# Latent attention heads: normalising the output rows instead of the exponentials, and moving the fp16 split from VectorE to ScalarE and GpSimd

## The chip, the core and the metric

The program runs on one core of one Trainium2 chip. A core has five engines with queues of their own, each strictly in order: TensorE (PE in the profile; its weight loads are shown apart as PEld), VectorE (DVE), ScalarE (ACT), GpSimd (POOL) and SyncE (SP), which here issues nearly all DMAs. They meet only at semaphores. The metric is the device time of one execution in microseconds. Before the change it is 1346.02 us, the median of three runs (1341.62 to 1346.54).

## The reference

One encoder layer over 1024 positions and 1024 channels: adaLN modulation, a mixer and a gated MLP. The mixer has 8 heads of banded attention and 8 heads of latent attention. The change touches the latent heads only, which compute (cut to that part):

```python
q = rmsnorm(q, g_mla_q[l]);  k = rmsnorm(k, g_mla_k[l])          # 96 wide per head
q = concat([q[..., :64], rope(q[..., 64:], positions)]);  k = ...
s = einsum('bqhd,bkhd->bhqk', qi, k) * scale
s = where(key_chunk <= q_chunk, s, NEG_INF)                       # chunks of 64
p = softmax(s, axis=-1)
o = einsum('bhqk,bkhd->bqhd', p, v)                               # v is 64 wide per head
```

## The kernel before

Products are kept near fp32 accuracy by splitting operands into a high and a low half and multiplying three of the four pairs. For the attention weights both halves are fp16.

A *unit* is one head and one half (g = 0 or 1) of the 1024 query positions; the 8 latent heads give 16 units, named m00_0 (group 0, head 0, half 0), m00_1, m01_0 and so on to m13_1. A unit has four *rows*, query tiles of 128 positions; row i (0 to 7 over both halves of a head) looks at n = 128(i+1) keys. So rows 0 to 3 (half 0) have n of 128 to 512 and are *short*; rows 4 to 7 (half 1) have n of 640 to 1024, and their weights are split in two *pieces*, the first of 512 columns, the second of 128 to 512.

A unit starts with its **pages** (`qk_page`, L700, called by `mla_unit`, L915): TensorE transposes four 128x96 tiles of q into one PSUM bank, ScalarE copies the high half out, VectorE subtracts for the low half; then the same for k. The bank is a tile with the tag "T", of which there is one buffer (`TB = 1`, L43; `page_psum`, L694). A new tile of a tag waits until the readers of the tile before it are done, in the order in which the source asks for them. The eight PSUM banks are taken: two score tiles "S" of two banks each, one "T", one "pv" and two "mm" for other products.

`Unit.scores` (L742) does one row: matmuls into an S tile; VectorE masks with a memset (L789) and takes the row minimum of the negated scores (L790); ScalarE forms the exponentials and their row sum in one pass (L797, with a second instruction that reads the accumulator). VectorE turns the sum into 2^15/sum (L799, L800). For each piece GpSimd multiplies the exponentials by that factor and writes the high fp16 half (L73, the helper `scale_pool`), VectorE forms exponential times factor minus high half as the low half (L819), and SyncE issues one DMA that transposes both halves into a PT tile (L831).

`Unit.values` (L836) runs for every second row, three rows (`DEPTH`) behind the scores: matmuls of the value tiles against the transposed weights into the bank "pv" (L859). After the last pair of a unit ScalarE and VectorE add the two 64-row halves and undo the power-of-two scales (L868, L869), and SyncE stores the output (L873).

`pace` fills in other products between rows: first the up-projection of the second group of heads (`f_up(1)`, L596), then the part of the output projection that belongs to the banded heads (`f_oca`, L674). The source asks for things in the order of the loop at L984. The final order of each engine's queue is made at build time by a list scheduler from that order, with priorities raised for the scores (`OFF_S`), the split (`OFF_P`) and the values (`OFF_V`); it is then fixed.

Of the kernel before, what the change touches and what calls it, by code (L numbers as in the profile page):

```python
# [13 lines left out]
F32 = mybir.dt.float32  # L14
# [4 lines left out]
AF = mybir.ActivationFunctionType  # L19
ALU = mybir.AluOpType  # L20
AX = mybir.AxisListType
# [3 lines left out]
P = 128  # L25
# [18 lines left out]
MODE_C = "1111"  # L44
MODE_M = "1111"
# [19 lines left out]
def layer_kernel(ctx, tc, I, out):  # L65
# [6 lines left out]
    def scale_pool(o, i, s):  # L72
        pool.tensor_scalar(o, i, s, 1.0, op0=MUL, op1=MUL)  # L73
# [241 lines left out]
    def pow2_scale(nm, ssw, b2, n, fac):  # L315
        t = cst.tile([P, 3, ND], F32, name=f"vs{nm}")
        dve.tensor_tensor(t[:, 0, :n], ssw, b2, op=MUL)
        pt = ps.tile([P, 512], F32, name=f"vsp{nm}", tag="mm", bufs=2)
        pe.matmul(pt[:, :n], ones[:], t[:, 0, :n], start=True, stop=True)
        dve.tensor_reduce(t[:, 1, 0:1], pt[:, :n], axis=AX.X, op=ADD)  # L320
        dve.tensor_scalar(t[:, 1, 0:1], t[:, 1, 0:1], fac, 1e-30, op0=MUL, op1=ADD)
        pool.tensor_tensor(t[:, 1, 1:2], t[:, 1, 0:1], nhalf[:], op=ALU.pow)
        ab = cst.tile([P, 2], F32, name=f"vab{nm}")
        dve.tensor_scalar(t[:, 2, 0:1].bitcast(I32), t[:, 1, 1:2].bitcast(I32), 0x7F800000, None, op0=ALU.bitwise_and)
        dve.reciprocal(t[:, 2, 1:2], t[:, 2, 0:1])
        dve.tensor_scalar(t[:, 2, 1:2], t[:, 2, 1:2], 1.0001, None, op0=MUL)
        dve.tensor_scalar(t[:, 2, 1:2].bitcast(I32), t[:, 2, 1:2].bitcast(I32), 0x7F800000, None, op0=ALU.bitwise_and)
        dve.tensor_scalar(ab[:, 0:1], t[:, 2, 0:1], VSCALE, None, op0=MUL)
        dve.tensor_scalar(ab[:, 1:2], t[:, 2, 1:2], 1.0 / (VSCALE * PSCALE), None, op0=MUL)
        return ab[:, 0:1], ab[:, 1:2]  # L330
# [265 lines left out]
    def f_up(gr):  # L596
# [19 lines left out]
        vscale["m", gr] = pow2_scale(f"m{gr}", ssw[:], gb2[:], 1, float(KVR))  # L616
# [117 lines left out]
    class Unit:  # L734
# [7 lines left out]
        def scores(u, i):  # L742
# [6 lines left out]
            rsum = cst.tile([P, 1], F32, name=f"rs{nm}", tag="rsum", bufs=4)  # L749
            ri = cst.tile([P, 1], F32, name=f"ri{nm}", tag="ri", bufs=4)  # L750
            with tc.high_priority(offset=OFF_S):
# [36 lines left out]
                else:  # L788
                    dve.memset(sv[0:64, n - 64:n], BIG)  # L789
                    anchor["dve"] = dve.tensor_reduce(m[:], sv, axis=AX.X, op=MIN).ins  # L790
# [7 lines left out]
            with tc.high_priority(offset=OFF_P):  # L798
                dve.reciprocal(ri[:], rsum[:, 0:1])  # L799
                dve.tensor_scalar(ri[:], ri[:], PSCALE, None, op0=MUL)  # L800
                for x, (p0, p1) in enumerate(pieces):
# [7 lines left out]
                    mode = (MODE_C if u.band else MODE_M)[cnt[0] % 4]  # L809
                    if mode == "2":  # L810
                        scale_pool(pp, pp, ri[:])
                        act.activation(hl[:, :w], pp, AF.Copy)
                        pool.tensor_tensor(hl[:, w:2 * w], pp, hl[:, :w], op=SUB)
                    else:
                        if mode == "1":
                            scale_pool(hl[:, :w], pp, ri[:])
                        else:
                            act.activation(hl[:, :w], pp, AF.Copy, scale=ri[:])
                        dve.scalar_tensor_tensor(hl[:, w:2 * w], pp, ri[:], hl[:, :w], op0=MUL, op1=SUB)  # L819
# [12 lines left out]
                    for j in range(w // P):  # L832
                        where.setdefault(lo + p0 // P + j, []).append((b0 + j, b0 + j + w // P, i % 2))
            return sum(3 * max(107, w / 2.4) for _, _, w, _ in segs)

        def values(u, i):  # L836
# [17 lines left out]
            with tc.high_priority(offset=OFF_V):  # L854
# [7 lines left out]
                if i % 4 == 3:  # L862
# [6 lines left out]
                    dve.scalar_tensor_tensor(dst[r0], u.pv[r0], inv[r0], dst[r0], op0=MUL, op1=ADD)  # L869
                    if final:  # L870
# [735 lines left out]
```

## Time and profile before

| | before |
|---|---|
| median of the runs | 1346.02 us |
| profiled execution | 1345.89 us, span 1344.1 us |
| mean granted TensorE clock | 0.946 |
| PE busy | 1223.8 us (91%), 6168 instructions |
| VectorE busy | 1096.2 us (82%), 1928 |
| ScalarE busy | 622.7 us (46%), 1132 |
| GpSimd busy | 578.1 us (43%), 610 |

Busy time of PE is modelled from pipelined instructions, so a busy PE is not PE at its peak. In a group of instructions "out<-in xcount | busy, mean ns | idle before, releaser" gives the tiles that are written and read, how many instructions there were, their total and mean duration, and how long the engine stood idle just before them and whose work ended that. The latent heads take up the stretch from about 400 to 630 us of the span; the banded heads lie before it, the output projection and the MLP behind it.

### The profile page before, as it was taken

To read this page: it belongs to the slowest core of one execution; us is meant where nothing else is said; L and a number is where in the kernel's file an instruction comes from. 1 tells how busy PE (TensorE), PEld (TensorE's weight loads), DVE (VectorE), ACT (ScalarE), POOL (GpSimd) and SP (SyncE) were. 2 spreads that over 40 slices of the span, in tenths; PEclk is the share of its full clock that TensorE was granted. 3 is DMA by queue.
4 is the path that set the end of the run, shared out by engine and by line. 5 is a ranking of instruction groups with operands and counts; after the bars stand their busy time and mean duration, and the time that the engine had idled before them with its cause. 6 is when DMAs were issued, how large, how long until landed. Compare 5 with 4: busy or idle time off the path is not lost.

```text
span 1344.1 us, 18696 instructions
## 1 busy us (share of the span) xinstructions
PE 1223.8 (91%) x6168; PEld 1003.8 (75%) x6168; DVE 1096.2 (82%) x1928; ACT 622.7 (46%) x1132; POOL 578.1 (43%) x610
## 2 busy tenths in 40 slices
PE   4899798998877798886998999999999998999998
PEld 3788587896655567765776888888888886888886
DVE  6978798864679987894989988988899997687667
ACT  4453546443555544563376444444434444433431
POOL 5464557565646763354634444444445431000000
PEclk9899798998787889996999999999999998999999
DMA  8415577854413477779911333333323326943441
GB/s 323 138 35 116 135 177 179 192 127 110 87 32 80 94 153 165 141 150 252 377 49 47 126 110 133 103 122 98 133 102 118 126 98 241 390 141 117 130 161 63
DMA packets 223689, 190.57 MB, mean 142 GB/s; under 512 B 148708, under 2 KB 166884, under 8 KB 223592
## 3 DMA queue, kind: packets, MB, share of 16 engines
q1 hardware_dynamic: 223592, 189.38, 49.1%
q8 instruction: 48, 0.79, 0.2%
q14 instruction: 49, 0.40, 0.1%
HBM read 117.24 MB, written 37.49 MB: 115 GB/s over the span
## 4 chain that ended last, share of the span: by engine, by line
PE 41%; DVE 10%; issue 3%; ACT 2%; DMA 1%; POOL 1%; SPq 0%; DVEq 0%; ACTq 0%; POOLq 0%
PE p L1082 7%; PE p L1084 7%; PE p L1083 7%; PE dnA_P L1417 2%; PE dnA_P L1419 2%; PE dnA_P L1418 2%; PE dnB_P L1419 1%; PE dnB_P L1418 1%; PE dnB_P L1417 1%; DVE u L1253 1%; DVE u L1254 1%; PE op L154 1%; PE dnA L1417 1%; PE dnA L1419 1%; PE dnA L1418 1%
## 5 line engine op out<-in xcount | busy, mean ns | idle before, releaser
L77 ACT ACTIVATE dnP<-dnr 128x1024 fp32r<-128x1024 f32 x73 | 77.5, 1064 | 117.5 <-PE dnA_P L1419 46.4
L1391 DVE TENSOR_TENSOR dnP<-dnr,dnP 128x1024 fp32r<-128x1024 f32 x72 | 87.9, 1223 | 52.6 <-ACT dnP L77 52.6
L73 POOL TENSOR_SCALAR hlm<-Pm,rim 128x512 f16<-128x512 f32 (+3 forms) x96 | 68.8, 726 | 83.5 <-DVE rim L800 22.3
L84 POOL TENSOR_TENSOR wf<-wu,wf 128x512 fp32r<-128x512 f32 x22 | 38.8, 1762 | 116.3 <-ACT wf L77 116.3
L1253 DVE SCALAR_TENSOR_TENSOR u<-c,cvp,u 128x1023 f32<-128x1023 f32 x44 | 64.8, 1513 | 27.8 <-ACT u L1252 27.8
L73 POOL TENSOR_SCALAR hlc<-Pc,ric 128x640 f16<-128x640 f32 (+2 forms) x64 | 50.8, 797 | 61.0 <-ACT Pc L797 20.8
L819 DVE SCALAR_TENSOR_TENSOR hlm<-Pm,rim,hlm 128x512 f16<-128x512 f32 (+3 forms) x96 | 68.0, 719 | 9.8 <-POOL hlm L73 9.7
L797 ACT ACTIVATE Pc<-sc,mc 128x640 f32<-128x640 f32 (+2 forms) x64 | 42.1, 658 | 53.1 <-DVE mc L786 35.9
L797 ACT ACTIVATE Pm<-sm,mm 128x128 f32<-128x128 f32 (+3 forms) x64 | 47.1, 736 | 41.7 <-DVE mm L790 24.2
L84 POOL TENSOR_TENSOR wb<-wu,wb 128x512 fp32r<-128x512 f32 x22 | 38.1, 1732 | 64.5 <-ACT wb L77 50.7
L1252 ACT ACTIVATE u<-c,cvp 128x1024 f32<-128x1024 f32 x44 | 52.3, 1237 | 27.8 <-DVE c L1351 19.2
L1254 DVE SCALAR_TENSOR_TENSOR u<-c,cvp,u 128x1022 f32<-128x1022 f32 x44 | 63.8, 1488 | 0.0
L859 PE MATMUL pvm<-PTm,vt 128*128 128x256 f16 (+1 forms) x320 | 45.7, 294 | 17.0 <-DMA PTm<-hlm 9.9
L819 DVE SCALAR_TENSOR_TENSOR hlc<-Pc,ric,hlc 128x640 f16<-128x640 f32 (+2 forms) x64 | 51.6, 809 | 9.3 <-POOL hlc L73 8.7
L155 PE MATMUL ipq<-wq_s,hT 128*128 128x256 f32 x192 | 56.0, 292 | 0.1
L859 PEld LDWEIGHTS <-vt 128*128 128x128 f16 x320 | 31.6, 109 | 32.7 <-DMA PTm<-hlm 15.0
L154 PE MATMUL ipq<-wq_s,hT 128*128 128x256 f32 x192 | 55.8, 293 | 0.0
L156 PE MATMUL ipq<-wq_s,hT 128*128 128x256 f32 x192 | 55.4, 289 | 0.0
L77 ACT ACTIVATE wc<-ws 128x512 fp32r<-128x512 f32 x21 | 13.3, 632 | 88.0 <-DVE ws L1101 82.2
L1418 PE MATMUL dnA_P<-dnP 128*128 128x512 f32 x132 | 51.4, 389 | 0.0
L1419 PE MATMUL dnA_P<-dnP 128*128 128x512 f32 x132 | 51.3, 389 | 0.0
L1417 PE MATMUL dnA_P<-dnP 128*128 128x512 f32 x132 | 51.2, 389 | 0.0
(442 smaller groups left out, 4428.4 us busy)
## 6 DMA issues: line engine op xcount, KB each, us to landing
wu<-w_up SPq DMA_DIRECT2D x44, 512.0 KB, 3.5
dnr<-g_d SPq DMA_DIRECT2D x73, 256.0 KB, 2.8
aw<-w_ada SPq DMA_DIRECT2D x48, 256.0 KB, 3.5
g_d<-u SPq DMA_DIRECT2D x22, 512.0 KB, 3.0
dnr<-w_down SPq DMA_DIRECT2D x44, 256.0 KB, 5.3
adaw<-w_ada_a SPq DMA_DIRECT2D x16, 512.0 KB, 6.3
x<-x SPq DMA_DIRECT2D x16, 512.0 KB, 9.0
g_d<-gs SPq DMA_DIRECT2D x22, 256.0 KB, 2.8
```

The source lines that it names most:

```text
L73: pool.tensor_scalar(o, i, s, 1.0, op0=MUL, op1=MUL)
L77: act.activation(o, i, AF.Copy)
L797: act.activation(pr[:, :n], sv, AF.Exp, bias=m[:], scale=-1.0, accum_out=rsum[:, 0:1])
L819: dve.scalar_tensor_tensor(hl[:, w:2 * w], pp, ri[:], hl[:, :w], op0=MUL, op1=SUB)
L1082: pe.matmul(pt, sh, pg[:, 0], start=(k == 0 and not add), stop=False, skip_group_check=skip)
L1083: pe.matmul(pt, sh, pg[:, 1], start=False, stop=False, skip_group_check=skip)
L1084: last = pe.matmul(pt, sl, pg[:, 0], start=False, stop=(k == 3), skip_group_check=skip)
L1253: dve.scalar_tensor_tensor(u[:, 1:], c[:, :S - 1], cvp[:, cv + 1:cv + 2], u[:, 1:], op0=MUL, op1=ADD)
L1391: r = f(*a, **k)
L1417: pe.matmul(pt, sh, w[:, 0, 0], start=start, stop=False, skip_group_check=add)
L1418: pe.matmul(pt, sh, w[:, 1, 0], start=False, stop=False, skip_group_check=add)
L1419: pe.matmul(pt, sl, w[:, 0, 0], start=False, stop=stop, skip_group_check=add)
```

## The change

The exponentials of the latent heads are no longer divided by their row sums before the split. The factor 2^15 is put into the exponent instead (ln 2^15 is added to the row minimum), and the division is done once per unit on the output. Four row sums of a unit are kept in one 128x4 tile, inverted in one instruction when the unit's fourth row is scored. At the end of the unit TensorE transposes each of the four columns, broadcast over 128 columns, into a PSUM tile `bc` of 128x512, so that every partition holds the 512 reciprocals along its columns; VectorE multiplies the output by it. That tile has the tag "T", the bank of the pages.

The split is shared out anew. First pieces of long rows: GpSimd copies the high half (a product with 1.0), VectorE subtracts. Short rows and second pieces: ScalarE copies the high half and GpSimd subtracts. The banded heads keep what they did.

```diff
-MODE_C = "1111"
-MODE_M = "1111"
...
-    def pow2_scale(nm, ssw, b2, n, fac):
+    def pow2_scale(nm, ssw, b2, n, fac, psc=PSCALE):
...
-        dve.tensor_scalar(ab[:, 1:2], t[:, 2, 1:2], 1.0 / (VSCALE * PSCALE), None, op0=MUL)
+        dve.tensor_scalar(ab[:, 1:2], t[:, 2, 1:2], 1.0 / (VSCALE * psc), None, op0=MUL)
...
-        vscale["m", gr] = pow2_scale(f"m{gr}", ssw[:], gb2[:], 1, float(KVR))
+        vscale["m", gr] = pow2_scale(f"m{gr}", ssw[:], gb2[:], 1, float(KVR), 1.0)
...
-            rsum = cst.tile([P, 1], F32, name=f"rs{nm}", tag="rsum", bufs=4)
-            ri = cst.tile([P, 1], F32, name=f"ri{nm}", tag="ri", bufs=4)
+            if u.band:
+                rsum = cst.tile([P, 1], F32, name=f"rs{nm}", tag="rsum", bufs=4)
+                ri = cst.tile([P, 1], F32, name=f"ri{nm}", tag="ri", bufs=4)
+            else:
+                if i % 4 == 0:
+                    u.rs = cst.tile([P, 4], F32, name=f"ru{nm}", tag="ru", bufs=3)
+                rsum = u.rs[:, i % 4:i % 4 + 1]
...
                     dve.memset(sv[0:64, n - 64:n], BIG)
-                    anchor["dve"] = dve.tensor_reduce(m[:], sv, axis=AX.X, op=MIN).ins
+                    dve.tensor_reduce(m[:], sv, axis=AX.X, op=MIN)
+                    anchor["dve"] = dve.tensor_scalar(m[:], m[:], math.log(PSCALE), None, op0=ADD).ins
...
-                dve.reciprocal(ri[:], rsum[:, 0:1])
-                dve.tensor_scalar(ri[:], ri[:], PSCALE, None, op0=MUL)
+                if u.band:
+                    dve.reciprocal(ri[:], rsum[:, 0:1])
+                    dve.tensor_scalar(ri[:], ri[:], PSCALE, None, op0=MUL)
...
-                    mode = (MODE_C if u.band else MODE_M)[cnt[0] % 4]
-                    if mode == "2":
-                        scale_pool(pp, pp, ri[:])
-                        act.activation(hl[:, :w], pp, AF.Copy)
-                        pool.tensor_tensor(hl[:, w:2 * w], pp, hl[:, :w], op=SUB)
+                    hi, lw = hl[:, :w], hl[:, w:2 * w]
+                    if u.band:
+                        scale_pool(hi, pp, ri[:])
+                        dve.scalar_tensor_tensor(lw, pp, ri[:], hi, op0=MUL, op1=SUB)
+                    elif len(pieces) == 2 and x == 0:
+                        scale_pool(hi, pp, 1.0)
+                        dve.tensor_tensor(lw, pp, hi, op=SUB)
                     else:
-                        if mode == "1":
-                            scale_pool(hl[:, :w], pp, ri[:])
-                        else:
-                            act.activation(hl[:, :w], pp, AF.Copy, scale=ri[:])
-                        dve.scalar_tensor_tensor(hl[:, w:2 * w], pp, ri[:], hl[:, :w], op0=MUL, op1=SUB)
+                        act.activation(hi, pp, AF.Copy)
+                        pool.tensor_tensor(lw, pp, hi, op=SUB)
...
+            if not u.band and i % 4 == 3:
+                dve.reciprocal(u.rs[:], u.rs[:])
...
                     dve.scalar_tensor_tensor(dst[r0], u.pv[r0], inv[r0], dst[r0], op0=MUL, op1=ADD)
+                    if not u.band:
+                        bc = ps.tile([P, 512], F32, name=f"bc{u.nm}_{u.g}", tag="T", bufs=TB)
+                        for b in range(4):
+                            pe.transpose(bc[:, b * P:(b + 1) * P], u.rs[:, b:b + 1].to_broadcast([P, P]), ident[:])
+                        dve.tensor_tensor(dst[r0], dst[r0], bc[r0], op=MUL)
```

## The prediction, made before the changed kernel was run

> **What bounds the kernel now.** The change lies in the latent heads, so I first cut the span into stretches. The columns are the stretch, its length, busy time and count of each engine, the granted TensorE clock, and the DMA share and rate.
>
> ```profile
> core 0: us, PE busy (x) PEld busy (x) DVE busy (x) ACT busy (x) POOL busy (x), PEclk, DMA share, GB/s
> 400.00:450.00 50.00, 36.33 (x156) 28.51 (x156) 46.06 (x140) 27.94 (x69) 34.48 (x34) 0.73 0.38 84
> 450.00:500.00 50.00, 40.58 (x210) 31.14 (x211) 46.53 (x127) 27.82 (x59) 33.66 (x35) 0.86 0.60 126
> 500.00:550.00 50.00, 45.46 (x265) 36.20 (x263) 39.71 (x100) 25.57 (x55) 20.35 (x29) 1.00 0.76 164
> 550.00:600.00 50.00, 44.50 (x263) 35.29 (x264) 42.65 (x114) 26.37 (x57) 21.70 (x29) 0.97 0.72 142
> ```
>
> From 400 to 600 us VectorE is busy 175 of 200 us. PE's busy time is long too, but it holds waits: at the granted clock of 0.73 it shows 36 of 50. The view of waits for 395 to 630 us and the chain of work over 380 to 660 us say who is waited for:
>
> ```profile
> by line: issue 4.6%; DVE hlm L819 3.3%; DMA PTm<-hlm 2.0%; PE op L154 1.8%; PE op L155 1.7%; DMA cl<-oT_d 1.5%; DVE mm L790 1.5%; PE op L156 1.4%; DMA wor<-w_out 1.4%; PE sm L771 1.2%; DVE om L869 1.1%; DMA oT_d<-om 0.8%; POOL ol L84 0.8%;
> ```
> ```profile
> ACT Pm L797 <- DVE mm L790: 24.2, 17, 3.5
> POOL hlm L73 <- DVE rim L800: 22.3, 12, 3.9
> ```
>
> ScalarE waits for the row minimum, GpSimd for the factor, and both are late because they stand in VectorE's queue. So VectorE sets the pace here. That pace is read off the outputs of the units, two rows of VectorE's timeline: the output of the unit m01_1, and that of the last one.
>
> ```profile
> 486.51 0.76 DVE L869 SCALAR_TENSOR_TENSOR om<-pvm,vabm,om 64x512 f32<-64x512 f32 x1
> ...
> 629.28 0.76 DVE L869 SCALAR_TENSOR_TENSOR om<-pvm,vabm,om 64x512 f32<-64x512 f32 x1
> ```
>
> Between them lie six heads: 142.8/6 = **23.8 us per head**.
>
> **The change part by part.** The prices come from the groups kept apart by shape over 395 to 630 us, and two rows of the page:
>
> ```profile
> L73 POOL TENSOR_SCALAR hlm<-Pm,rim 128x512 f16<-128x512 f32 (+3 forms) x96 | 68.8, 726 | 83.5 <-DVE rim L800 22.3
> ...
> L819 DVE SCALAR_TENSOR_TENSOR hlm<-Pm,rim,hlm 128x512 f16<-128x512 f32 (+3 forms) x96 | 68.0, 719 | 9.8 <-POOL hlm L73 9.7
> ```
> ```profile
> L819 DVE SCALAR_TENSOR_TENSOR hlm<-Pm,rim,hlm 128x512 f16<-128x512 f32 x48 | 43.1, 897 | 6.9 <-POOL hlm L73 6.8
> ...
> L73 POOL TENSOR_SCALAR hlm<-Pm,rim 128x512 f16<-128x512 f32 x48 | 41.6, 868 | 61.2 <-DVE rim L800 14.5 <-DVE sm L789 10.5 <-ACT Pm L797 8.4
> ...
> L797 ACT ACTIVATION_READ_ACCUMULATOR Pm<-sm,mm 128x1 f32 x64 | 12.5, 195 | 0.0
> ...
> L84 POOL TENSOR_TENSOR cl<-cl,ch 128x512 fp32r<-128x512 f32 x8 | 11.8, 1476 | 4.0 <-ACT ch L77 4.0
> L869 DVE SCALAR_TENSOR_TENSOR om<-pvm,vabm,om 64x512 f32<-64x512 f32 x16 | 11.7, 734 | 1.4 <-ACT om L868 1.1
> ...
> L710 DVE SCALAR_TENSOR_TENSOR mk<-mk_ps,gk_m,mk 96x512 fp32r<-96x512 f32 x16 | 11.6, 724 | 2.2 <-ACT mk L709 2.1
> ...
> L868 ACT ACTIVATE om<-pvm,vabm 64x512 f32<-64x512 f32 x16 | 10.9, 683 | 6.9 <-PE pvm L859 6.0 <-DMA oT_d<-om 0.7
> L709 ACT ACTIVATE mk<-mk_ps,gk_m 96x512 fp32r<-96x512 f32 x16 | 10.9, 681 | 10.0 <-PE mk_ps L697 9.4 <-PE sm L771 0.5
> ...
> L790 DVE TENSOR_REDUCE mm<-sm 128x1 f32<-128x1024 f32 x8 | 9.7, 1215 | 0.1
> L799 DVE RECIPROCAL rim<-rsm 128x1 f32<-128x1 f32 x64 | 9.7, 151 | 4.5 <-ACT Pm L797 4.3
> L77 ACT ACTIVATE wo<-wor 128x512 fp32r<-128x512 f32 x16 | 9.6, 624 | 11.7 <-DMA wor<-w_out 10.2 <-PE oc L156 1.2 <-PE qu L156 0.2
> ...
> L800 DVE TENSOR_SCALAR rim<-rim 128x1 f32<-128x1 f32 x64 | 9.2, 143 | 0.5
> ...
> L797 ACT ACTIVATE Pm<-sm,mm 128x1024 f32<-128x1024 f32 x8 | 8.9, 1109 | 3.9 <-DVE mm L790 2.5 <-DVE rim L800 1.4
> L790 DVE TENSOR_REDUCE mm<-sm 128x1 f32<-128x896 f32 x8 | 8.7, 1084 | 0.1
> ...
> L790 DVE TENSOR_REDUCE mm<-sm 128x1 f32<-128x768 f32 x8 | 7.6, 951 | 0.1
> ...
> L706 DVE TENSOR_TENSOR mq_1l<-mq_ps,mq_1h 96x512 fp32r<-96x512 f32 x8 | 5.4, 673 | 0.2
> ...
> L705 ACT ACTIVATE mq_1h<-mq_ps 96x512 fp32r<-96x512 f32 x8 | 4.7, 591 | 7.5 <-PE mq_ps L697 7.5
> ```
>
> *VectorE.* Gone: 68.0 (L819) + 9.7 (L799) + 9.2 (L800) = 86.9 us. New: 32 subtracts at 0.897 as before = 28.7 (the plain subtract of L706, 0.673, would make 21.5); 64 additions of ln 2^15 priced by L800, 9.2; 16 reciprocals, 2.4; 16 output products priced by L869, 11.7. Together 52.0, so VectorE loses **35 us** (42 by the other price), 4.4 per head.
>
> *ScalarE* gets 64 copies of 128 to 512 columns, at most 0.624 each: under 40 us on 108 busy of 200. *GpSimd* loses 64 of its 96 products and gets 64 subtracts. The nearest row is 1.476 at 512 columns; by columns the 64 (mean 320) cost about 59 us, and 32 x 0.868 = 28 remain: 87 against 68.8. Neither engine fills up: their room is 92 and 90 us in these 200. *TensorE* gets 64 transposes, four for 0.60 us as in the first row below: 9.6 us. *SyncE* keeps its 96 transposing DMAs; two thirds are now released by GpSimd instead of VectorE. The set-up edit (`psc`) changes a constant and costs nothing.
>
> If work on the engines were all, the stage would gain. **The bank "T" is why I expect otherwise.** The transposed reciprocals are a third use of that one buffer, asked for between the pages of two units: pages of unit u, `bc` of u-1, pages of u+1. It comes free only when VectorE has multiplied the finished output of u-1. So unit u+1 can't even begin its pages before the output of u-1 is whole; before, pages waited for pages only. The built order of TensorE shows it. Before, the pages of m02_0 and m02_1 stand ahead of all values of m01_0; after, each unit's q page stands behind the last values of the unit two earlier, and VectorE's queue has the product of m10_1 right ahead of the low half of m11_1's q page. This makes a ring that is closed once per head: q page of half 1, k page, rows 4 to 7, values, output, q page of the next head's half 1. Its length follows from a stretch of the timeline, and the landing time of the transposes:
>
> ```profile
> 560.31 0.60 PE L697 MATMUL mq_ps<-ident,qn 128*96 128x128 f32 x4
> ...
> 560.67 0.94 PE L771 MATMUL sm<-mk,mq_1h 96*128 96x512 f32 x4
> ...
> 561.45 0.51 PE L771 MATMUL sm<-mk,mq_1l 96*128 96x512 f32 x2
> ...
> 563.00 0.80 DVE L790 TENSOR_REDUCE mm<-sm 128x1 f32<-128x640 f32 x1
> ...
> 563.89 0.80 ACT L797 ACTIVATE Pm<-sm,mm 128x640 f32<-128x640 f32 x1 [2.21 <-DVE mm L790]
> ...
> 565.55 0.94 PE L859 MATMUL pvm<-PTm,vt 128*128 128x256 f16 x8
> ```
> ```profile
> DMA to landing us min/median/max: 2.3/3.1/4.6
> ```
>
> - q page: 0.60 + 0.591 + 0.673 = 1.86; k page: 0.60 + 0.681 + 0.724 = 2.00
> - the part of the scores of rows 4 and 5 that needs the new k page, about one row's six matmuls (560.67 to 561.96): 1.29
> - VectorE then has, in its new order, the minima of rows 4 and 5, the other half's output product and the addition: 0.80 + 0.951 + 0.734 + 0.143 = 2.63
> - exponential of row 4, which frees an S tile: 0.80 + 0.195 = 1.00; scores of row 6: 1.29
> - minima of rows 6 and 7 and an addition: 1.084 + 1.215 + 0.143 = 2.44
> - VectorE's order has row 6's subtract ahead of row 7's addition. Row 6's exponential runs beside row 7's minimum; GpSimd's copy and the subtract follow: 0.868 + 0.897 + 0.143 = 1.91
> - exponential of row 7: 1.109 + 0.195 = 1.30; ScalarE's copy and GpSimd's subtract of its second piece: 0.624 + 1.476 = 2.10
> - transpose 3.1, eight value matmuls 0.94, output: 0.683 + 0.734 + 0.734 = 2.15
>
> Sum: 24.0 us. Each of some 28 steps is handed over at about 0.09 us (from the minimum's end at 563.80 to the exponential at 563.89): 2.5, so 26.5. In the queues other work stands ahead: the values of half 0 and their output step between the q and the k page, and on ScalarE a page copy and a filler's copy ahead of row 7's exponential, 0.6 to 0.7 each. With half to all of four such items the ring is 27.8 to 29; where the overlaps are better than I wrote them, it is 24 to 26. I take **27 us**, near the sum with handovers. VectorE's need, 23.8 - 4.4 = 19.4, lies under that, so its relief becomes idle time.
>
> Six heads at 27 instead of 23.8 are +19 us. For the first two (400 to 486 us) I take no change: they hold the up-projection's VectorE work, lose 2 x 4.4 = 9 there, and pay for the same ring with that work standing in it; bounds -9 and +10. Against the profiled execution: 1345.9 + 19 = **1365 us**. Its own time is 0.1 us under the median of the three runs, so nothing is corrected. The forecast's own range has the ring from 25 to 30 us, 1353 to 1383, and a little of the first heads' loss on top: 1353 to 1386.
>
> **Rivals.**
> *A, the relief reaches the end.* If the ring is mostly hidden, heads run at VectorE's new need with today's gaps: 8 x 4.4 = 35 us less, 1311. Between that and the forecast lies the bare ring, 24.0 per head, with 9 us won in the first heads: 1345.9 + 1 - 9 = 1338. For it speaks that VectorE is busy 93% in the first two rows; against it that even the bare sum doesn't go under 23.8. A case faster by over 0.5% needs handovers near nothing and the first heads' gain. It decides from a ring under 24 us.
> *B, it cancels.* Ring 24 to 25.5 and a gain in the first heads: 1340 to 1352.
> *C, the clock falls as well.* In the rows above the granted clock is 0.73 where PE was busy 36 of 50 us and 1.00 where it was busy 45. If the ring leaves TensorE idle for stretches, its steps in the ring (0.60 twice, 1.29 twice, 0.94: 4.7 us) could take up to twice as long: +4.7 on six heads, 28 more, 1393. [...]
> *D, GpSimd is the new bound.* Its subtract in the MLP stage takes longer than 1.476:
>
> ```profile
> L84 POOL TENSOR_TENSOR wf<-wu,wf 128x512 fp32r<-128x512 f32 x22 | 38.8, 1762 | 116.3 <-ACT wf L77 116.3
> ```
>
> At 1.762 the 64 cost 70 us and each ring 0.3 more: 1367. It doesn't change the sign, so it is kept within the forecast.
>
> **How the numbers follow.** Forecast 0.52, C 0.08, B 0.14, A 0.26. Half a per cent, 6.7 us, is about what a measurement of this kernel can tell from none. So slower by over 0.5%: 0.52 + 0.08 = 0.60; within: 0.14; faster: 0.26. The range for eight in ten goes from 1334, which takes in the bare ring and half of A's milder part, to 1386, the upper end of the forecast; C's far end and A's relief stay out.
>
> **What would show it.** Right: VectorE's busy time in the latent heads falls by 35 to 42 us, yet outputs come 26 to 29 us apart per head; TensorE stands at the first transpose of q pages, released by the output's product; the clock over 500 to 600 is lower than 0.97. Wrong: a head in under 24 us, pages that never wait for an output, or an end of the latent heads before 620 us. ScalarE or GpSimd over 90% busy would show that I mis-sized what they took over.

## The result, and the profile after

| | before | after |
|---|---|---|
| median of four runs each | 1344.99 us | 1403.91 us (1400.98 to 1407.68) |
| ratio | 1 | **1.0448**, 95% interval 1.0423 to 1.0473 |
| profiled execution, span | 1345.89, 1344.1 us | 1400.98, 1399.2 us |
| mean granted TensorE clock | 0.946 | 0.938 |

The changed kernel is 4.5% slower. The direction was forecast, the size was not: 1365 us was predicted, with 1386 as the upper end. These are the page's first lines for the kernel after:

```profile
span 1399.2 us, 18776 instructions
...
PE 1250.7 (89%) x6232; PEld 1023.3 (73%) x6232; DVE 1068.1 (76%) x1832; ACT 649.0 (46%) x1196; POOL 587.3 (42%) x610
```

VectorE has 28 us less work than before (1096.2), and the kernel takes 55 us more. Where those went is read off the outputs of the units in VectorE's timeline of the kernel after: half 1 of head m01, half 1 of the head behind it, and the last output.

```profile
487.42 0.76 DVE L875 SCALAR_TENSOR_TENSOR om<-pvm,vabm,om 64x512 f32<-64x512 f32 x1 [8.61 <-ACT om L874]
...
529.11 0.74 DVE L875 SCALAR_TENSOR_TENSOR om<-pvm,vabm,om 64x512 f32<-64x512 f32 x1 [0.52 <-ACT om L874]
...
690.97 0.76 DVE L875 SCALAR_TENSOR_TENSOR om<-pvm,vabm,om 64x512 f32<-64x512 f32 x1 [9.36 <-ACT om L874]
```

Up to 487 us the two kernels stand level (486.51 before). The six heads behind take 203.6 instead of 142.8 us: **33.9 us per head instead of 23.8**. The last output is 61.7 us late (690.97 against 629.28), and 6.6 of them come back behind it, since the rest of the span is 708.2 instead of 714.8 us. In the table of windows of the kernel after (length; busy us and instructions of PE, PEld, DVE, ACT, POOL; granted clock; DMA share; GB/s) no engine but PE is busy for much more than half the time, and PE's busy time is stretched by the lower clock (in the turn below four transposes take 1.09 us at a granted clock of 0.50, and 0.60 at 1.00):

```profile
500.00:550.00 50.00, 37.66 (x173) 28.80 (x172) 25.26 (x57) 21.79 (x47) 15.70 (x19) 0.79 0.50 105
550.00:600.00 50.00, 39.70 (x210) 30.58 (x210) 25.12 (x60) 24.36 (x55) 17.29 (x21) 0.87 0.53 111
```

VectorE is idle half of the time, and the granted clock has fallen from 1.00 and 0.97 to 0.79 and 0.87. A stage in which no engine is full is held by a chain of steps that wait for one another. The waits of the kernel after, 395 to 690 us (time in all, times, longest), name the place where the predicted ring closes, TensorE at the first transpose of a q page until VectorE's product is done:

```profile
PEld mq_ps L695 <- DVE om L880: 8.8, 4, 2.7
...
PE mq_ps L695 <- DVE om L880: 7.6, 4, 2.4
```

The two rows are the weight loads and the matmuls of the same transposes, so they overlap: some 9 us, little beside 61.7. In a ring every engine waits for its neighbour, and the wait that closes it is only one of some 28; what the ring costs has to be found by following it round. One turn, from the output product of m10_1 (its end, 594.84) to that of m11_1 (626.29), in the timeline of the kernel after:

```profile
594.16 0.68 DVE L880 TENSOR_TENSOR om<-om,bcm 64x512 f32<-64x512 f32 x1
...
595.96 0.60 PE L695 MATMUL mq_ps<-ident,qn 128*96 128x128 f32 x4
...
597.21 0.69 DVE L704 TENSOR_TENSOR mq_1l<-mq_ps,mq_1h 96x512 fp32r<-96x512 f32 x1 [2.37 <-ACT mq_1h L703]
...
597.76 0.94 PE L865 MATMUL pvm<-PTm,vt 128*128 128x256 f16 x8 [1.21 <-DMA PTm<-hlm]
598.51 1.16 PE L774 MATMUL sm<-mk,mq_1h 96*128 96x512 f32 x4
...
599.51 0.60 PE L695 MATMUL mk_ps<-ident,kn 128*96 128x128 f32 x4
...
600.87 0.75 DVE L708 SCALAR_TENSOR_TENSOR mk<-mk_ps,gk_m,mk 96x512 fp32r<-96x512 f32 x1 [0.66 <-ACT mk L707]
...
602.97 1.64 DVE L793 TENSOR_REDUCE mm<-sm 128x1 f32<-128x640 f32 x2
604.64 0.69 DVE L880 TENSOR_TENSOR om<-om,bcm 64x512 f32<-64x512 f32 x1
605.36 0.21 DVE L794 TENSOR_SCALAR mm<-mm 128x1 f32<-128x1 f32 x2
...
605.38 1.09 PE L695 MATMUL mq_ps<-ident,qn 128*96 128x128 f32 x4 [2.09 <-DVE om L880]
605.63 0.79 ACT L801 ACTIVATE Pm<-sm,mm 128x640 f32<-128x640 f32 x1 [4.80 <-DVE mm L794]
...
606.57 1.86 PE L774 MATMUL sm<-mk,mq_1h 96*128 96x512 f32 x4
...
608.23 0.95 PE L774 MATMUL sm<-mk,mq_1l 96*128 96x512 f32 x2
...
609.39 0.69 DVE L704 TENSOR_TENSOR mq_0l<-mq_ps,mq_0h 96x512 fp32r<-96x512 f32 x1
...
610.24 1.09 DVE L793 TENSOR_REDUCE mm<-sm 128x1 f32<-128x896 f32 x1
...
611.66 1.22 DVE L793 TENSOR_REDUCE mm<-sm 128x1 f32<-128x1024 f32 x1
...
613.39 0.91 POOL L823 TENSOR_TENSOR hlm<-Pm,hlm 128x384 f16<-128x384 f32 x1
613.44 1.41 DVE L820 TENSOR_TENSOR hlm<-Pm,hlm 128x512 f16<-128x512 f32 x1 [0.55 <-POOL hlm L71]
614.77 0.14 DVE L794 TENSOR_SCALAR mm<-mm 128x1 f32<-128x1 f32 x1
...
614.95 1.11 ACT L801 ACTIVATE Pm<-sm,mm 128x1024 f32<-128x1024 f32 x1 [0.58 <-DVE mm L794]
615.96 0.19 ACT L801 ACTIVATION_READ_ACCUMULATOR Pm<-sm,mm 128x1 f32 x1
...
616.70 0.63 ACT L75 ACTIVATE ch<-cl 128x512 fp32r<-128x512 f32 x1 [0.55 <-DMA cl<-oT_d]
617.24 0.61 ACT L822 ACTIVATE hlm<-Pm 128x512 f16<-128x512 f32 x1
617.41 1.37 POOL L82 TENSOR_TENSOR cl<-cl,ch 128x512 fp32r<-128x512 f32 x1 [0.56 <-ACT ch L75]
...
618.74 2.18 POOL L823 TENSOR_TENSOR hlm<-Pm,hlm 128x512 f16<-128x512 f32 x3
...
623.12 0.94 PE L865 MATMUL pvm<-PTm,vt 128*128 128x256 f16 x8 [0.84 <-DMA PTm<-hlm]
...
625.60 0.69 DVE L880 TENSOR_TENSOR om<-om,bcm 64x512 f32<-64x512 f32 x1
```

Against the prediction's terms (each from the end of the step before it to its own end, so handovers are in the measured column):

| step of the ring | taken | measured |
|---|---|---|
| wait for TensorE before the q page (other products) | – | 1.12 |
| q page | 1.86 | 1.94 |
| wait before the k page (values of half 0, whose transposes land late, and scores behind them) | – | 1.61 |
| k page | 2.00 | 2.11 |
| rest of the scores of rows 4 and 5 | 1.29 | 1.35 |
| minima, the other half's product, addition | 2.63 | 2.60 |
| exponential of row 4 | 1.00 | 1.00 |
| scores of row 6 | 1.29 | **2.61** |
| wait before row 6's minimum (half 0's q page on VectorE) | – | 1.06 |
| minima of rows 6 and 7, addition | 2.44 | 2.64 |
| copy and subtract of row 6, addition | 1.91 | 2.03 |
| exponential of row 7 | 1.30 | 1.24 |
| copy, subtract of the second piece, transpose | 5.20 | **6.97** |
| values, output, product | 3.09 | 3.17 |
| sum | 24.0, with handovers and items 27 | **31.45** |

The plain steps came out within 0.6 us of the sum. What is missing is in five places, 6.9 us together: three waits for an engine that is doing something else (3.8), scores at half the rate (1.3), and a tail in which ScalarE's and GpSimd's pieces of another product (616.70, 617.41) stand ahead of row 7's (1.8).

### The profile page after: what moved, and what is told of

The parts are those of the page before. It is cut to its first block, busy times and chain, and to the rows that moved or that the text cites. A ratio compares the mean times of both kernels' runs of the same rounds, so it can differ in the third digit from the quotient of the medians.

```text
span 1399.2 us, 18776 instructions
## 1 busy us (share of the span) xinstructions
PE 1250.7 (89%) x6232; PEld 1023.3 (73%) x6232; DVE 1068.1 (76%) x1832; ACT 649.0 (46%) x1196; POOL 587.3 (42%) x610
## 5 line engine op out<-in xcount | busy, mean ns | idle before, releaser
L82 POOL TENSOR_TENSOR wb<-wu,wb 128x512 fp32r<-128x512 f32 x22 | 45.3, 2060 | 81.4 <-ACT wb L75 55.1
L1264 DVE SCALAR_TENSOR_TENSOR u<-c,cvp,u 128x1023 f32<-128x1023 f32 x44 | 56.1, 1317 | 27.8 <-ACT u L1263 26.5
L865 PE MATMUL pvm<-PTm,vt 128*128 128x256 f16 (+1 forms) x320 | 46.0, 294 | 29.2 <-DMA PTm<-hlm 25.1
L823 POOL TENSOR_TENSOR hlm<-Pm,hlm 128x384 f16<-128x384 f32 (+2 forms) x64 | 54.3, 854 | 32.6 <-ACT hlm L822 26.6
L1263 ACT ACTIVATE u<-c,cvp 128x1024 f32<-128x1024 f32 x44 | 52.4, 1238 | 24.3 <-DVE c L1362 17.4
L71 POOL TENSOR_SCALAR hlm<-Pm 128x512 f16<-128x512 f32 x32 | 22.2, 696 | 89.6 <-ACT Pm L801 82.8
L774 PE MATMUL sm<-mk,mq_1h 96*128 96x512 f32 (+3 forms) x128 | 43.9, 463 | 14.2 <-ACT Pm L801 5.3
L1265 DVE SCALAR_TENSOR_TENSOR u<-c,cvp,u 128x1022 f32<-128x1022 f32 x44 | 56.5, 1324 | 0.0
L1429 PE MATMUL dnA_P<-dnP 128*128 128x512 f32 x132 | 51.4, 390 | 0.0
L1430 PE MATMUL dnA_P<-dnP 128*128 128x512 f32 x132 | 51.4, 389 | 0.0
```

What stands on the lines that cost most here:

```text
L82: (pool if eng == "p" else dve).tensor_tensor(o, i, f32(hi), op=SUB)
L865: last = pe.matmul(dst, u.vst(j), mov, start=(x == 0), stop=(x == len(todo) - 1), skip_group_check=True)
L1265: dve.scalar_tensor_tensor(u[:, 2:], c[:, :S - 2], cvp[:, cv:cv + 1], u[:, 2:], op0=MUL, op1=ADD)
L1429: pe.matmul(pt, sh, w[:, 1, 0], start=False, stop=False, skip_group_check=add)
L1430: pe.matmul(pt, sl, w[:, 0, 0], start=False, stop=stop, skip_group_check=add)
```

## The experiments

Medians and ratios are against the kernel before on the same chip (1341.6 to 1343.1 us). "Per head" is the time from the output of m01_1 to the last output, over six: 23.8 us before, 33.9 after.

**1. The division left out.** From the kernel after, the transposes, the product and their bank request are taken out.

```diff
-                    if not u.band:
-                        bc = ps.tile([P, 512], F32, name=f"bc{u.nm}_{u.g}", tag="T", bufs=TB)
...
-                        dve.tensor_tensor(dst[r0], dst[r0], bc[r0], op=MUL)
```


> The changed kernel without the transposed reciprocals and without the product on the outputs (the division by the row sums is left out; everything else of the change stays, the new shares of the split among it). Ring theory (units are chained by the one buffer of the tag T): pages run ahead again, heads come 19.4 to 24 us apart instead of 33.9, time 1310 to 1345 us. Rival (the new split by ScalarE and GpSimd is what is slow): the heads stay above 30 us apart and the time above 1385 us.

Measured: 1344.63 us, ratio 1.0008 (0.9990 to 1.0025). The loss is gone, so all else in the change costs nothing by itself. But nothing is won either. In the windows of this run VectorE is busy 31 of 50 us, where it was busy 39.7 before, and its heads take 24.3 us, from 485.19 to 631.07:

```profile
500.00:550.00 50.00, 43.40 (x258) 35.27 (x256) 31.35 (x75) 32.52 (x70) 22.78 (x27) 0.97 0.73 146
```
```profile
485.19 0.76 DVE L875 SCALAR_TENSOR_TENSOR om<-pvm,vabm,om 64x512 f32<-64x512 f32 x1
...
631.07 0.76 DVE L875 SCALAR_TENSOR_TENSOR om<-pvm,vabm,om 64x512 f32<-64x512 f32 x1 [8.81 <-ACT om L874]
```

**2. The reciprocals in another bank.** The whole change, with `bc` in the two banks of the other products.

```diff
-                        bc = ps.tile([P, 512], F32, name=f"bc{u.nm}_{u.g}", tag="T", bufs=TB)
+                        bc = ps.tile([P, 512], F32, name=f"bc{u.nm}_{u.g}", tag="mm", bufs=2)
```


> The changed kernel with the transposed reciprocals in the tag mm (two buffers, shared with the filler products) instead of T; nothing else. Ring theory: the pages no longer wait for outputs; fillers do, but they have slack: 1315 to 1360 us, with the 64 transposes and 16 products in it. Rival (the transposes and products themselves, or the split, are what costs): 1385 us or more.

Measured: 1347.15 us, ratio 1.0034 (1.0010 to 1.0058). One line of the source is worth 55 of the 59 us of loss. The heads take 22.9 us here, but the first ones end later (m01_1 at 494.06), because, as I read the source, their reciprocals then stand among the up-projection's products in those banks.

**3. The old split, with the new division.** In the kernel after, all pieces get GpSimd's copy and VectorE's subtract.

```diff
-                    elif len(pieces) == 2 and x == 0:
+                    else:
                         scale_pool(hi, pp, 1.0)
                         dve.tensor_tensor(lw, pp, hi, op=SUB)
-                    else:
-                        act.activation(hi, pp, AF.Copy)
-                        pool.tensor_tensor(lw, pp, hi, op=SUB)
```


> The changed kernel with the old shares in the split: GpSimd copies every high half and VectorE subtracts every low half, nothing on ScalarE; division at the output as in the change. Ring theory: still slow, 1390 to 1425 us, as each ring has the same steps with VectorE in the place of ScalarE and GpSimd. Rival (ScalarE and GpSimd in the split are the cost): 1340 to 1360 us.

Measured, one run: 1402.46 us, 33.2 us per head. With the ring in place, how the split is shared out doesn't matter.

**4. The ring alone.** The kernel before, with its division as it was, plus only a `bc` of ones in the bank T and the product with it.

```diff
+                    if not u.band:
+                        bc = ps.tile([P, 512], F32, name=f"bc{u.nm}_{u.g}", tag="T", bufs=TB)
+                        for b in range(4):
+                            pe.transpose(bc[:, b * P:(b + 1) * P], ones[:, b:b + 1].to_broadcast([P, P]), ident[:])
+                        dve.tensor_tensor(dst[r0], dst[r0], bc[r0], op=MUL)
```


> The kernel before with one thing added: at the end of each latent unit four transposes of a column of ones into a tile of the tag T, and the output multiplied by it (so the outputs are unchanged). Division, split and shares as before. Ring theory: the chain of units alone makes it 1390 to 1430 us, since it has the longer VectorE path per row too. Rival (the ring is not it): only the added work counts, 16 products and 64 transposes, 12 us of VectorE: 1350 to 1360 us.

Measured, one run: 1404.81 us. Its last output in VectorE's timeline is that of the kernel after, to 2 us:

```profile
689.34 0.76 DVE L869 SCALAR_TENSOR_TENSOR om<-pvm,vabm,om 64x512 f32<-64x512 f32 x1 [7.49 <-ACT om L868]
```

So the third use of the one bank makes the whole loss, without any other part of the change. It is spread differently: m01_1 comes at 498.26 us, 11.8 later than before, and the six heads behind it take 31.8 us each instead of 33.9. With experiments 1 and 2 that settles the cause from both sides.

**5. The bank held for a shorter time.** `bc` is made ahead of a unit's last values and copied by ScalarE to SBUF, so that T is free before the output is there.

```diff
+                    bc = ps.tile([P, 512], F32, name=f"bc{u.nm}_{u.g}", tag="T", bufs=TB)
...
+                    rb = atile(f"rb{u.nm}_{u.g}")
+                    act.activation(rb[:], bc[:], AF.Copy)
...
-                        dve.tensor_tensor(dst[r0], dst[r0], bc[r0], op=MUL)
+                        dve.tensor_tensor(dst[r0], dst[r0], rb[r0], op=MUL)
```


> The changed kernel with the transposed reciprocals made ahead of the unit's last values and copied out of T by ScalarE at once, so that T is held for one transpose group and one copy instead of until the output is whole. Ring theory: the ring now closes at the exponential of a unit's last row, about 16 to 20 us per head, shorter than the 23 to 24 us that TensorE's work takes, so 1335 to 1360 us. Rival (any third use of T costs like this): 1385 us or more.

Measured: 1375.52 us, ratio 1.0254 (1.0216 to 1.0293), 28.1 us per head. The expectation was too low. 34 of the 59 us of loss are left. By the source the copy still waits for the last row sum of the unit, so the ring is shorter by its tail (transpose, values, output) and not open; I didn't follow a turn of it.

**6. T for the first head, mm behind it.** This avoids what experiment 2 lost at the start.

```diff
+                        tg, nb_ = ("T", TB) if u.nm == "m00" else ("mm", 2)
```


> The changed kernel with the transposed reciprocals of the first head in T and those of the other seven in mm. In the run with all of them in mm the first head's second output came at 474 us against 445 (it stood behind the up-projection in mm), while the later heads came 22.9 us apart. If both halves hold: second head done by 488 us, six heads at 22.9, 1330 to 1343 us. Rival (the late heads only caught up what the first had lost; TensorE's work sets the end): 1343 to 1352 us.

Measured: 1343.21 us, ratio 1.0014 (0.9995 to 1.0032). It is the best form of the change, and no faster than the kernel before. The first head's second output comes at 450.35 us, against 474.02 in experiment 2, and m01_1 at 490.35. But the six heads then take 23.8 us each and not 22.9: as the rival said, those of experiment 2 had in part caught up what the first had lost.

**7. What lengthens the ring.** Two items of the table come from the output projection of the banded heads. It is put behind the last latent unit; in a second run six more score matmuls per row, into a bank that nobody reads, keep TensorE busy.

```diff
     def pace(cost, ratio):
+        if fillers and fillers[0][0] == "oca":
+            return
```
The second run has this behind the scores of a row as well (cut):

```diff
+                if not u.band and (u.nm, u.g) not in (("m00", 0), ("m00", 1), ("m01", 0)):
+                    wm = ps.tile([P, 512], F32, name=f"wm{nm}", tag="mm", bufs=2)
+                    for _ in range(6 // len(segs)):
...
+                            last = pe.matmul(wm[:, :w], qpg[0][rs_, q], kpgs[kh][rs_, 0, ko:ko + w], start=True, stop=True)
```


> The changed kernel with no filler products (the banded heads' part of the output projection) between the rows of the latent heads; they run after the last unit. The ring stays. If the fillers standing ahead of ring steps in the queues (their loads, copies and subtracts on ScalarE and GpSimd, their products on TensorE) stretched the ring from 27 to 33 us, heads come 26 to 29 us apart; if it was TensorE's clock, which falls further without fillers, they stay at 32 us or more. Total time 1390 to 1440 us in either case, since about 45 us of products now run alone.

> The changed kernel without fillers between the rows, with six extra matmuls per row from the second head's second half on, into a tile of mm that nobody reads (they repeat score products). Without them the heads came 33.2 us apart at a granted clock of 0.70 to 0.76. If the low clock is what made the ring longer than the 27 us of the prediction, the clock goes above 0.9 and heads come 26 to 30 us apart although TensorE has more to do; if not, 33 us or more. Total time 1400 to 1450 us.

Measured, one run each: 33.1 us per head without the products, 33.5 with the matmuls added (whole times 1447.36 and 1448.28, in which the products come later). The table of windows, run without and run with the matmuls:

```profile
550.00:600.00 50.00, 33.92 (x155) 24.83 (x153) 24.95 (x53) 19.15 (x40) 10.30 (x15) 0.70 0.38 70
```
```profile
550.00:600.00 50.00, 40.86 (x213) 32.26 (x213) 23.56 (x50) 18.63 (x40) 11.62 (x14) 0.80 0.40 72
```

Taking away the other products didn't shorten the ring, nor did raising the clock. The second run doesn't clear the clock wholly: it came up only in part, to 0.80 to 0.93, and the added matmuls take time in TensorE's queue themselves. In the run without the products the wait ahead of the q page is gone, yet the one ahead of the k page has grown from 1.6 to 4.6 us (q page whole at 556.56, k page begun at 561.18):

```profile
555.87 0.69 DVE L704 TENSOR_TENSOR mq_1l<-mq_ps,mq_1h 96x512 fp32r<-96x512 f32 x1 [1.46 <-ACT mq_1h L703]
557.89 1.68 PE L865 MATMUL pvm<-PTm,vt 128*128 128x256 f16 x8 [2.69 <-DMA PTm<-hlm]
559.32 2.06 PE L774 MATMUL sm<-mk,mq_1h 96*128 96x512 f32 x4
...
561.18 0.85 PE L695 MATMUL mk_ps<-ident,kn 128*96 128x128 f32 x4
```

Of the 4.6 us, 1.3 are a wait for half 0's transposes to land. The rest is half 0's values and four score matmuls, which take 1.68 and 2.06 us here. They took 0.94 and 1.16 in the turn followed above, where the granted clock was 1.00; here its mean over 550 to 600 us is 0.70. So where one item went, the late landing and a slower TensorE took its room. That half 0 is late because the ring makes it late is likely and not shown.

**8. Is TensorE the limit without the ring?** In runs on the kernel of experiment 2 and on the kernel before, one of the three products of each term of that output projection is left out.

```diff
-            pe.matmul(pt, sh, ml, start=False, stop=False)
+            if not two:
+                pe.matmul(pt, sh, ml, start=False, stop=False)
```


> The kernel with the reciprocals in mm, and one of the three products of the banded heads' part of the output projection left out (64 matmuls of 512 columns, 15 us of TensorE at 0.235 each; the low half of one operand is left out of the result); nothing else is lighter. If TensorE's queue is what sets the pace of the latent heads once VectorE is relieved, 8 to 17 us less than with them: 1330 to 1340 us. If VectorE, ScalarE or a DMA sets it, within 4 us of 1347.

> The kernel before with one of the three products of the banded heads' part of the output projection left out (64 matmuls, 15 us of TensorE; the low half of one operand is missing from the result). If TensorE's queue set the pace of the latent heads before the change, 8 to 17 us less than before: 1325 to 1336 us. If VectorE did, as the prediction said, or something that neither engine touches, within 4 us of before.

Measured: 1347.78 us (ratio 1.0044, 1.0029 to 1.0059) on the changed kernel, 1339.93 us (0.9980, 0.9964 to 0.9997) on the kernel before. Neither gains more than about 3 us. But leaving work out also lowered the clock: over 495 to 605 us it was 0.89 and 0.91, where it had been 0.98 in both kernels, and PE's busy time fell by only 4.3 and 4.7 us of 110. So these runs bound what TensorE's work is worth; they don't exclude it.

**9. Are the transposing DMAs?** On the kernel of experiment 2 only the high halves are transposed and read twice; then both savings together.

```diff
-                        anchor["sp"] = sp.dma_start_transpose(tt[:, b0:b0 + 2 * w // P, :], hl[:, :2 * w]).ins
+                        wt_ = 2 * w if u.band else w
+                        anchor["sp"] = sp.dma_start_transpose(tt[:, b0:b0 + wt_ // P, :], hl[:, :wt_]).ins
...
-                        where.setdefault(lo + p0 // P + j, []).append((b0 + j, b0 + j + w // P, i % 2))
+                        where.setdefault(lo + p0 // P + j, []).append((b0 + j, b0 + j + (w // P if u.band else 0), i % 2))
```


> The kernel with the reciprocals in mm, with only the high halves of the latent heads' weights transposed by DMA (half the columns per transfer) and used in the place of the low halves too (the low halves are left out of the result); TensorE has as many matmuls as there, the split is still computed. If the arrival of the transposes is what keeps the heads at 23 us once VectorE is relieved and T is free, the heads come 18 to 21 us apart and the time is 1315 to 1335 us; if not, within 5 us of 1347.

> Both edits on the kernel with the reciprocals in mm: only the high halves transposed, and one product of the banded heads' output projection left out (both left out of the result). If TensorE and the transposes bind together, this gains 15 us or more where each alone gains nothing: 1310 to 1330 us. If a third thing sets the pace (the two score tiles, or ScalarE's order), within 5 us of 1347.

Measured: 1353.79 us (1.0078, 1.0049 to 1.0107) and 1347.89 us (1.0039, 1.0017 to 1.0062); 23.5 us per head in both. The first is 7 us above 1347, outside both branches; nothing is gained in either. The DMA share fell from 0.74 to 0.45 in the first (495 to 605 us). So the amount moved isn't the limit. The issuing of these DMAs wasn't tested: each of them holds SyncE's queue (SPq) about as long as before. The rows of the PT tiles over 495 to 605 us, kernel before and first run (shortest, median and longest in ns):

```profile
L831 SPq DMA_TRANSPOSE PTm<-hlm x57: 1167/1252/1997, 493.9 to 604.8; - x57
```
```profile
L836 SPq DMA_TRANSPOSE PTm<-hlm x56: 1113/1209/2489, 498.1 to 604.3; - x56
```

By count and median that is an estimated 71 and 68 us of the 110, in one queue.

**10. Is it VectorE at all?** The products between the rows are put behind the last unit, as in 7, on the kernel of experiment 2 and on the kernel before.

> The reciprocals in a bank of the mm products, and the other products of TensorE (output projection of the banded heads) all put behind the last latent unit, so the whole time grows and only the latent heads count: the time from the output of m01_1 to the last output, over six. With the other products between the rows it was 22.9 us per head. Theory (rows' own chain over two score tiles and three engines sets the pace): 21.5 to 24 per head, with VectorE busy under 38 of 50 us. Rival (the other products between the rows fill what VectorE's relief gave): 20 or less.

> The kernel before with the same products put behind the last latent unit. Heads 23.8 us with them. If VectorE sets the pace of the kernel before, as the prediction said, taking away products of TensorE that need little VectorE leaves 22.5 us or more, with VectorE busy over 42 of 50 us. If the products themselves hold the pace: 21 or less. If the rows' chain does: as in the run with the reciprocals in mm, within 1 us of it.

Measured: 21.8 and 22.0 us per head (whole times 1379.94 and 1384.94). First the run with the relief, then the kernel before, windows and last outputs:

```profile
550.00:600.00 50.00, 38.88 (x233) 29.82 (x233) 36.29 (x90) 31.53 (x72) 22.11 (x29) 0.90 0.62 119
```
```profile
550.00:600.00 50.00, 38.61 (x212) 29.46 (x213) 42.15 (x115) 22.98 (x51) 20.33 (x28) 0.86 0.68 124
```
```profile
490.85 0.76 DVE L875 SCALAR_TENSOR_TENSOR om<-pvm,vabm,om 64x512 f32<-64x512 f32 x1 [0.48 <-ACT om L874]
...
621.46 0.76 DVE L875 SCALAR_TENSOR_TENSOR om<-pvm,vabm,om 64x512 f32<-64x512 f32 x1 [10.07 <-ACT om L874]
```
```profile
487.68 0.76 DVE L869 SCALAR_TENSOR_TENSOR om<-pvm,vabm,om 64x512 f32<-64x512 f32 x1 [0.40 <-ACT om L868]
...
619.63 0.76 DVE L869 SCALAR_TENSOR_TENSOR om<-pvm,vabm,om 64x512 f32<-64x512 f32 x1 [6.79 <-ACT om L868]
```

The products cost 1 to 2 us per head, at a clock that again fell (0.89 and 0.82 over 495 to 605 us). VectorE busy 36 or 42 of 50 us goes with 0.2 us of difference. The two runs differ in ScalarE too, busy 31.5 or 23.0 of 50 us, so a relief of VectorE by itself wasn't tried; but VectorE's relief as this change makes it gains nothing.

**11. Are the two score tiles?** Rows of up to 512 columns, from head m02 on, take their scores into the two mm banks: on the kernel of experiment 6 with the products in place, and on the kernel of experiment 2 without them.

```diff
-                s = ps.tile([P, 1024], F32, name=f"s{nm}", tag="S", bufs=2)
+                if u.band or i > 3 or u.nm in ("m00", "m01"):
+                    s = ps.tile([P, 1024], F32, name=f"s{nm}", tag="S", bufs=2)
+                else:
+                    s = ps.tile([P, 512], F32, name=f"s{nm}", tag="mm", bufs=2)
```


> The whole change with the reciprocals in T for the first head and in mm after it, and the short rows' score tiles in the two mm banks, with the other products where they were; complete. If the score tiles are the limit: under 1332 us (ratio under 0.992). If they are not, or the other products need those two banks: 1340 to 1355 us, heads at 23.5 us or more.

> As the run with the reciprocals in mm and no products between rows, and the short rows (at most 512 columns) of units from head m10 on and of m02 and m03 take their score tiles from the two mm banks, so that long and short rows don't share two tiles any more. If the two score tiles are what holds the rows' chain: 3 us per head less than without it, or more. If not: within 1 us.

Measured: 1374.67 us (1.0224, 1.0192 to 1.0257), 28.2 us per head; without the products 30.8 per head (1431.64). Both are slower than any branch allowed. I read it as the same fault again: reciprocals, which wait for an output, and scores, which the next output needs, now share the mm banks. So the same edit was made on the kernel before, which has no reciprocals to share with.

> The kernel before, undivided exponentials and reciprocals left out of it altogether, with the short rows' score tiles in the two mm banks from head m02 on. There is no output product here, so no ring of the kind that the run with four score tiles had (heads 28.2 us there, since its reciprocals and its short rows shared the two mm banks). If the two score tiles hold the heads at 23.8 us: 1325 us or less. If the other products then wait for these banks in turn: 1345 to 1375 us. If neither: within 6 us of before.

> The same with the other products put behind the last latent unit, so that the mm banks serve the short rows alone; only the heads count, and stand beside 22.0 us per head of the kernel before with these products behind it. If the two score tiles are the limit of the rows: 19 us or less. If the fixed order of the queues and the steps from row to row are: 21 to 23 us.

Measured: 1356.38 us (1.0098, 1.0061 to 1.0134), 25.6 us per head; without the products 26.1 per head (1403.80), where 22.0 stood before the edit. Shorter by 2.6 and 4.7 us per head than the two runs with reciprocals, which fits that reading, but no gain. The first lies in the branch in which the products wait for these banks. The second has neither products nor reciprocals there and still takes 4.1 us more per head than without the edit, against both its branches; why is open. So more score tiles, given to rows by their length, don't help, and whether the two tiles bind stays unsettled. A third tile for all rows wasn't tried; it would need two banks beside the eight that the kernel's tiles hold.

## Why the prediction was right in sign and wrong in size

- **The ring as mechanism: right.** Experiment 4 makes the whole loss with it alone; 1, 2 and 6, where the bank isn't shared so (6 only for one head), lose nothing or 0.3%.
- **The ring's length: this step failed.** The prediction took 27 us per head. Measured are 31.45 us in the turn that was followed, 32.4 over the last five heads (161.9/5) and 33.9 over all six. Its own steps, 24.0, were right to 0.6 us, handovers included, so the 2.5 that it added for these were hardly there. The term that failed is the one for other work in the queues: handovers and such items together were taken at 3.0 us and measured 7.4, of which 6.9 lie in five places. Of its four items of 0.6 to 0.7 only the values of half 0 cost time in the turn followed (within the 1.61); the other three were done before the ring came to them. Three places it hadn't listed: products ahead of the q page (1.12), half 0's q page on VectorE (1.06), and another product's pieces ahead of row 7's second piece (1.8). The fifth, the half rate (1.3), it held as rival C. In two of the five the work ahead itself waits, for a landing transpose or for a DMA of other products, which a price by the instructions' durations leaves out. Experiment 7 names no one item as the cause. Six heads at 27 gave +19 us; six at 33.9 are +60.8 on the outputs. Of the 42 that are missing, 27 lie in the last five heads and 15 in the first.
- **The first of the six heads** took 41.7 us (29.8 before), 9.3 more than the later ones and 10.3 more than the turn followed. Of the 10.3, 6.0 lie ahead of its q page: the product waits 2.9 us behind the whole output (488.18 to 491.12), and the q page another 4.2 (1.12 in the turn followed), while twelve matmuls of the banded heads' output projection run. Without these products, in experiment 7, the same head took 32.7 us. The rest wasn't taken apart.

```profile
491.12 0.69 DVE L880 TENSOR_TENSOR om<-om,bcm 64x512 f32<-64x512 f32 x1 [0.24 <-PE bcm L879]
```
```profile
496.01 0.60 PE L695 MATMUL mq_ps<-ident,qn 128*96 128x128 f32 x4
```

- **"VectorE sets the pace": not borne out.** It was the busiest engine beside TensorE, and waits pointed at it. But experiment 1 relieves it and gains nothing, and experiment 10 shows 21.8 against 22.0 us per head at two loads. Hence rival A, 35 us, had its chance from a bound that didn't show: with no ring at all the time is that of before. The terms of the relief were right: subtracts 29.2 us (28.7 taken), additions 8.9 (9.2), products 0.68 each (0.73). VectorE's total fell by 28 us and not by 35, so other instructions took 7 longer in all.
- **The first two heads: the number right, in part by luck.** Nothing was taken, as a gain of 9 against a ring of the same size, and their last output moved by 0.9 us. But the ring alone made it 11.8 us late (experiment 4), and the change without the ring 1.3 us early (experiment 1): the relief gained nearly nothing there by itself, and some 11 us where the ring was.
- **ScalarE, GpSimd (rival D): right.** Both end far from full, 25 and 21 us of 50 as means over 400 to 650 us. GpSimd's subtract took 1.26 us at 512 columns where 1.48 was taken.
- **Rival C, the clock: it came in part.** The granted clock fell to 0.79 to 0.87, and row 6's six matmuls took 2.61 us for 1.29, at a granted clock of 0.50. In the turn followed that is 1.3 us beyond the sum, and the plain steps, TensorE's others among them, lost 0.6 together, against the 4.7 that the rival charged. The second run of experiment 7 raised the clock in part, with matmuls that take time themselves, and didn't shorten the ring. No row that the prediction gives shows steps that take up to twice as long; in the kernel before four transposes took 1.05 us at 418.50, at a clock of 0.50 (416 to 420 us), and 0.60 at 426.21, at 1.00 (424 to 428 us).
- **Signs named in advance:** busy VectorE down while heads get longer, TensorE standing at the q pages, and a clock under 0.97 all showed. "26 to 29 us per head" did not.

What holds the heads at 22 to 24 us without a ring stays open. VectorE's relief as this change makes it and the amount transposed are ruled out; less work on TensorE gained at most 2 us per head, with the clock falling as well, and a split of score tiles by row length made it slower. Not tried by themselves are the order of the queues, the steps from row to row, and SyncE's queue, which the transposes alone hold for an estimated 71 of 110 us.

The form of experiment 6 is as fast as the kernel before (1.0014), and no complete version of the change beat it.

## What to carry to other kernels

Ask of every new use of a one-buffer tile what has to be finished before it comes free, and what has to wait for that: if the answer leads from one unit's output to a later unit's input, units that overlapped now run one after the other, and here no engine's relief paid for it. Price such a ring by what each engine does in the meantime, waits included, and not by the durations of the instructions ahead. And before the busiest engine is called the bound, ask whether a stage slows down when that engine is loaded or speeds up when it is relieved; a run that leaves the work out tells, if its granted clock is read beside its time.

## What the runs showed of the hardware

- TensorE's granted clock fell after a stretch that PE filled only in part. Four transposes took 1.09 us at 605.38, behind a wait of 2.1 us that begins at 603.29, and 0.60 at 599.51. In the windows of the kernel after PE is busy for 0.94 and 1.29 of 2.00 us while the clock is 1.00; then the clock is 0.53, and 0.50 for the next 4 us, in which PE is busy for 1.91 and 2.00 of 2.00 us:

```profile
600.00:602.00 2.00, 0.94 (x6) 0.63 (x5) 0.96 (x2) 0.68 (x1) 0.00 (x0) 1.00 0.00 0
602.00:604.00 2.00, 1.29 (x9) 0.96 (x8) 1.17 (x4) 0.00 (x0) 0.00 (x0) 1.00 0.00 0
604.00:606.00 2.00, 0.61 (x3) 0.60 (x4) 1.51 (x4) 0.37 (x1) 0.00 (x0) 0.53 0.00 0
606.00:608.00 2.00, 1.91 (x7) 1.29 (x6) 0.69 (x1) 2.00 (x7) 1.08 (x2) 0.50 0.30 66
608.00:610.00 2.00, 2.00 (x7) 1.71 (x6) 1.51 (x2) 0.37 (x2) 1.90 (x3) 0.50 0.43 83
610.00:612.00 2.00, 2.00 (x9) 1.59 (x8) 1.89 (x6) 0.39 (x1) 0.00 (x0) 0.77 0.96 180
```

  Whether the part-filled stretch set off the fall no run here shows.
- VectorE's subtract of 512 columns took 1.41 us at 613.44, where a GpSimd subtract of 384 columns began 0.05 us earlier and ran to 614.30, 0.55 us before VectorE's end. The mean of the 32 is 0.92, the median 0.69. Five more that began 0.05 to 0.07 us behind such a GpSimd subtract took 1.39 to 1.41 us. Why they took longer no run here shows.
